# Two softmaxes without a step between maximum and exponential, and a later first product with the values

## The chip, the cores and the metric

The kernel runs on one core of one Trainium2 chip. The metric is device time in microseconds (us), from the start of one execution to its end. Three runs of the kernel before took 3143.63, 3155.43 and 3157.5 us; the median is 3155.43 us.

## The reference, cut to what matters

The model is an encoder of two layers over 1024 tokens of width 1024, all in float32. Each layer has two attention branches from one modulated input, a gated merge of them, and a channel mixer. Only the two softmaxes and their products with the values matter here.

```python
# branch A: neighbourhood attention, 8 heads of 64, window of 8 rows x 16 columns, learned bias
s = jnp.einsum('bhcd,ibhcjd->bhcij', q_r, k_nb).astype(jnp.float32) * scale      # scale = 64 ** -0.5 = 0.125
s = s + bias.transpose(0, 2, 1, 3)[None].astype(jnp.float32)
p = jax.nn.softmax(s.reshape(B, H, GRID_W, kh * kw), axis=-1)
out = jnp.einsum('bhcij,ibhcjd->bhcd', p, v_nb)

# branch B: latent attention, 8 heads, every token against all 1024 keys
q = (rmsnorm(c_q, g_q) @ w_uq).reshape(B, S, H, MLA_NOPE_DIM + MLA_ROPE_DIM)
s = (jnp.einsum('bhqd,bkhd->bhqk', qn_b, k_nope) + jnp.einsum('bhqr,bkr->bhqk', qr_b, k_r))
p = jax.nn.softmax(s.astype(jnp.float32) * scale, axis=-1)                      # scale = 96 ** -0.5
out = jnp.einsum('bhqk,bkhd->bqhd', p, v)
```

## The kernel before, in words

Each layer runs in stages: the projections; branch A with the gate products between its units; branch B; the merge; the output projection; the mixer. TensorE (PE) does all products. Most are in three parts, high and low halves of operands split by ScalarE (ACT) and VectorE (DVE) (`split`, L200; `mm3`, L204).

**Branch A** (`na_steps`, L541) has 64 units a layer, one for 128 queries of one head. `unit_a` (L595) makes 128 x 384 scores in PSUM (tile `sna`, two products, L601). One DVE operation (L605) adds the table of biases and takes the row maximum; a second, small one (L607) multiplies the maximum by -0.125; ACT takes the exponential with it as bias and leaves the row sum (L608); DVE inverts the sum (L609) and GpSimd (POOL) multiplies the tile by it (L610). `unit_b` (L613), called two units later, turns the tile in three transposes on PE (L618, `pTna`) and copies it out of PSUM, on DVE (L621) for one half of the units and on ACT (L623) for the other; there are 7 buffers for the copies. `unit_c` (L626) multiplies the values by the copies, 64 output rows for each of two heads (L632, `pona`). It is called twice after every fourth unit, so four copies feed one block of 12 products. A product of these plain float32 operands stands as two MATMUL rows in the trace: a block is 24 rows.

**Branch B** (`mla_steps`, L646) has 64 units a layer as well. `unit_a` (L790) makes 128 x 1024 scores in six products (L796, `smla`; two PSUM buffers), takes the row maximum on DVE (L798), multiplies it by minus the scale in a small DVE operation (L799), and takes the exponential on ACT with that bias and the scale (L801); then follow the inverse (L802, DVE) and the product with it (L803, POOL). `unit_b` (L806), three units later in the program, turns the tile in two times four transposes (L815, `pTm`), copied by ACT (L821) and DVE (L819) into a `PT` tile, of which there are three; two units share one. `unit_c` (L823) multiplies the values by two `PT` tiles, one for each head: 16 products (L830, `pom`), 32 MATMUL rows, for four units and so eight copies. Here too each product writes 64 rows of the output, the heads in turn.

The order of each engine's instructions is not the order of the program. A planner lays them out ahead of time by a model of durations: of the instructions whose inputs are ready in the model, it takes the one that stands first in the program. A product of a block enters PE's order when its own copy is done in that model, whether or not the other copies of the block are.

Of the kernel before, what the change touches and what calls it, by code (L numbers as in the profile page):

```python
# [13 lines left out]
ALU = mybir.AluOpType  # L14
# [23 lines left out]
def hybrid_trunk(  # L38
# [161 lines left out]
    def split(dst_hi, dst_lo, src, pin=lambda ins: ins):  # L200
        pin(A.copy(dst_hi, src))  # L201
        V.tensor_tensor(dst_lo, src, dst_hi.bitcast(F32), op=ALU.subtract)  # L202

    def mm3(ps, terms, first=True, **kw):  # L204

        n = len(terms)
        for i, (wh, wl, mh, ml) in enumerate(terms):
            T.matmul(ps, wh, mh, start=first and i == 0, stop=False, **kw)  # L208
            T.matmul(ps, wh, ml, start=False, stop=False, **kw)  # L209
            T.matmul(ps, wl, mh, start=False, stop=i == n - 1, **kw)  # L210
# [144 lines left out]
    ada_sum(acc0, first_shift[:5], 0, pin)  # L355
    turn_rows(ta, na_, 0)
    turn_rows(tb, nb_, 128)

    ada_turn(0, 1, acc1)
    last = ada_sum(acc0, first_shift[5:], 5, pin)  # L360
# [180 lines left out]
    def na_steps(l, h):  # L541

        tabs = {}
        for hd in range(2):
            for rg in range(2):
                t = pool["na"].tile([P, 12, 96], F32, name=nm(f"tab{hd}{rg}"))
                G.memset(t, NEG)
                tabs[hd, rg] = t

        def tables(pair, hd, rg):  # L550
            for r in range(8):
                row = 8 * rg + r
                st = min(max(row - 4, 0), 8)
                d0 = st - row + 7
                k0 = st - 4 * rg
                nc.sync.dma_start(tabs[hd, rg][r * 16:(r + 1) * 16, k0:k0 + 8, :], u_d[2 * pair + hd, :, d0:d0 + 8, :])

        st, vts = {}, {}

        def qk_weights(pair, n):  # L560
            st["w"] = whalves(kblock(w_in[l], (4 * n + pair) * P))

        def qk_unit(pair, n, ch):
            if ch == 0:
                st[pair, n] = [slab("st", dt=F32R) for _ in range(2)]
            ps = dense(st["w"], h[ch])
            for hd in range(2):
                dst = st[pair, n][hd][:, cs(ch)]
                if n == 0:
                    view = lambda t: t.rearrange("p (g r c) -> p r g c", g=4, c=16)  # L570
                    stacks(dst, ps[:].rearrange("p (r g c) -> p r g c", g=4, c=16), hd, view)
                else:
                    stacks(dst, ps, hd)

        def k_swap(pair):
            st[pair, 2] = [slab("st", dt=F32R) for _ in range(2)]
            for hd in range(2):
                swapped(st[pair, 2][hd], st[pair, 1][hd])

        def values(pair):  # L580
            vt = []
            for wi, w in enumerate(NA_WIN):
                if wi % 2 == 0:
                    vs = slab("vna", (P, 2, 4, P))
                for blk in range(4):
                    nc.sync.dma_start(
                        vs[:, wi % 2, blk, :],
                        v_d[:].rearrange("(b r c) d -> b r c d", r=4, c=64)[blk, :, w:w + 32, pair * P:(pair + 1) * P],
                    )
                vt.append(vs[:, wi % 2])  # L590
            vts[pair] = vt

        pts, po = {}, {}

        def unit_a(pair, rg, cg, hd):  # L595
            q1, k1, k2 = (st[pair, n][hd] for n in range(3))
            w = NA_WIN[cg]
            ps = pool["na_ps"].tile([P, 12, 32], F32, tag="S", name=nm("sna"))
            qs = q1[:, rg * CH + cg * P:rg * CH + (cg + 1) * P]
            for i, kk in enumerate((k1, k2)):  # L600
                T.matmul(ps, qs, kk[:].rearrange("p (r c) -> p r c", c=64)[:, 4 * rg:4 * rg + 12, w:w + 32],  # L601
                         start=i == 0, stop=i == 1)
            pt = pool["na"].tile([P, 12, 32], F32, tag="P", name=nm("pna"), bufs=4)
            sm = small()
            V.tensor_tensor_reduce(pt, ps, tabs[hd, rg][:, :, NA_KIND[cg] * 32:(NA_KIND[cg] + 1) * 32],  # L605
                                   op0=ALU.add, op1=ALU.max, scale=1.0, scalar=-3e38, accum_out=sm[:, 0:1])
            V.tensor_scalar(sm[:, 1:2], sm[:, 0:1], -0.125, None, op0=ALU.mult)  # L607
            A.activation(pt, pt, AF.Exp, bias=sm[:, 1:2], scale=0.125, accum_out=sm[:, 2:3])  # L608
            V.reciprocal(sm[:, 3:4], sm[:, 2:3])  # L609
            G.tensor_scalar(pt, pt, sm[:, 3:4], 1.0, op0=ALU.mult, op1=ALU.mult)  # L610
            pts[pair, rg, cg, hd] = pt

        def unit_b(pair, rg, cg, hd):  # L613
            pt = pts[pair, rg, cg, hd]
            pT = bank("pTna")
            pf = pt[:].rearrange("p a b -> p (a b)")
            for j in range(3):
                T.transpose(pT[:, j * P:(j + 1) * P], pf[:, j * P:(j + 1) * P], ident)  # L618
            t = pool["na"].tile([P, 384], F32, tag="pT", name=nm("ptna"), bufs=7)
            if (cg + hd) % 2:  # L620
                V.tensor_copy(t, pT[:, :384])  # L621
            else:
                A.copy(t, pT[:, :384])  # L623
            pts[pair, rg, cg, hd] = t

        def unit_c(pair, rg, cg):  # L626
            if cg == 0:
                po[pair, rg] = pool["na_ps"].tile([P, CH], F32, tag="po", name=nm("pona"))
            p = po[pair, rg]
            for j in range(3):  # L630
                for hd in range(2):
                    T.matmul(p[64 * hd:64 * hd + 64, cg * P:(cg + 1) * P],  # L632
                             vts[pair][cg][:, j + rg, 64 * hd:64 * hd + 64],
                             pts[pair, rg, cg, hd][:, j * P:(j + 1) * P], start=j == 0, stop=j == 2)
            if cg == 3:
                o = tmp("ona")
                V.tensor_copy(
                    o[:].rearrange("p (r g c) -> p r g c", g=4, c=16),
                    p[:].rearrange("p (g r c) -> p r g c", g=4, c=16),
                )  # L640
                nc.sync.dma_start(o_d[pair * P:(pair + 1) * P, cs(rg)], o)

        return qk_weights, qk_unit, k_swap, values, tables, unit_a, unit_b, unit_c


    def mla_steps(l):  # L646
# [138 lines left out]
                stacks(st[pair, hd][1][:, cs(ch)], ps, hd)  # L785
                swapped(st[pair, hd][2][:, cs(ch)], st[pair, hd][1][:, cs(ch)])

        pts, pTs, po = {}, {}, {}

        def unit_a(pair, q2, hd, qi):  # L790
            q1, k1, k2, qr = st[pair, hd]
            t = slice(q2 * 256 + qi * P, q2 * 256 + (qi + 1) * P)
            ps = pool["S"].tile([P, 1024], F32, tag="S", name=nm("smla"))
            for ch in range(2):
                for i, (a, b) in enumerate(((q1, k1), (q1, k2), (qr, d["Kr"]))):
                    T.matmul(ps[:, cs(ch)], a[:, t], b[:, cs(ch)], start=i == 0, stop=i == 2)  # L796
            sm = small()
            V.reduce_max(sm[:, 0:1], ps, axis=AX.X)  # L798
            V.tensor_scalar(sm[:, 1:2], sm[:, 0:1], -MLA_SCALE, None, op0=ALU.mult)  # L799
            pt = pool["mla"].tile([P, 1024], F32, tag="P", name=nm("pmla"), bufs=5)  # L800
            A.activation(pt, ps, AF.Exp, bias=sm[:, 1:2], scale=MLA_SCALE, accum_out=sm[:, 2:3])  # L801
            V.reciprocal(sm[:, 3:4], sm[:, 2:3])  # L802
            G.tensor_scalar(pt, pt, sm[:, 3:4], 1.0, op0=ALU.mult, op1=ALU.mult)  # L803
            pts[pair, q2, hd, qi] = pt

        def unit_b(pair, q2, hd, qi):  # L806
            pt = pts[pair, q2, hd, qi]
            if qi == 0:
                pTs[pair, q2, hd] = pool["mla_t"].tile([P, 8, 256], F32, tag="PT", name=nm("PT"), bufs=3)
            pT = pTs[pair, q2, hd]  # L810
            for g in range(2):
                pb = bank("pTm")
                for j in range(4):
                    kk = 4 * g + j
                    T.transpose(pb[:, j * P:(j + 1) * P], pt[:, kk * P:(kk + 1) * P], ident)  # L815
                dst = pT[:, 4 * g:4 * g + 4, qi * P:(qi + 1) * P]
                src = pb[:].rearrange("p (a b) -> p a b", b=P)
                if g:
                    V.tensor_copy(dst, src)  # L819
                else:  # L820
                    A.copy(dst, src)  # L821

        def unit_c(pair, q2, half, o):  # L823
            if half == 0:
# [2 lines left out]
            for kk in range(4 * half, 4 * half + 4):  # L827
                for hd in range(2):
                    h = 2 * pair + hd
                    T.matmul(p[64 * hd:64 * hd + 64, :256], vm[kk][:, h * 64:(h + 1) * 64], pTs[pair, q2, hd][:, kk, :],  # L830
                             start=kk == 0, stop=kk == 7)
            if half == 1:
                t = slice((q2 % 2) * 256, (q2 % 2 + 1) * 256)
                if pair == 3:
# [711 lines left out]
```

## Time and profile before

| | us |
|---|---|
| median of three runs | 3155.43 |
| profiled execution | 3154.83 |
| its span | 3153.0 |
| PE busy | 3033.6 (96%) |
| PE weight loads busy | 2456.0 (78%) |
| DVE busy | 2069.4 (66%) |
| ACT busy | 1471.2 (47%) |
| POOL busy | 373.0 (12%) |

The profiled execution is 0.6 us under the median, and 1.8 us of it lie outside the span. PE has most work in every stage. The ends of its instructions are modelled and overlap, so the distance from one start to the next tells more than a duration: a row of 0.65 us may be followed 0.57 us after its start. Rows of the view by time merge neighbours of one kind; x30 is thirty MATMUL rows in a run without another kind between them.

### The profile page before, as it was taken

The page shows a single profiled execution, that of the slowest core. Times are in us where ns is not written, and L with a number is a line of the kernel's source. Part 1 is how long each engine was busy: PE and PEld are TensorE (multiplying, and loading weights), DVE is VectorE, ACT ScalarE, POOL GpSimd, SP SyncE. Part 2 cuts the span into 40 slices and gives each one's busy share as a digit, 9 for nine tenths or more (in the row PEclk, how much of TensorE's full clock was granted, in tenths as well). Part 3 has the DMA queues.
Part 4 walks back from the last instruction along what each step waited for, and adds up shares of the span by engine and source line. Part 5 has one row for each costly group of instructions (what it writes and reads, how often), then busy time and mean ns, then how long its engine had stood idle before and what let it go on. Part 6 is the DMA issues. An engine that isn't in the chain of part 4 may idle for free. (4 is left out here: it accounts for less than half of the span.)

```text
span 3153.0 us, 43333 instructions
## 1 busy us (share of the span) xinstructions
PE 3033.6 (96%) x15104; PEld 2456.0 (78%) x15104; DVE 2069.4 (66%) x3911; ACT 1471.2 (47%) x2820; POOL 373.0 (12%) x518
## 2 busy tenths in 40 slices
PE   7999999999998999999989999999999999999998
PEld 6878886776786888888777788777777778888887
DVE  8534436767859776877774334466775697767775
ACT  6234446554127666433352444555522466663332
POOL 5111002232200000000011011123221000000000
PEclk9999999999999999999999999999999999999999
DMA  6554334214853656856334444431266255586652
GB/s 258 157 135 111 99 109 119 63 36 145 280 191 107 244 207 231 293 196 209 106 121 138 125 121 114 117 86 36 73 214 218 69 180 214 211 308 205 215 166 84
DMA packets 359540, 497.56 MB, mean 158 GB/s; under 512 B 30556, under 2 KB 238618, under 8 KB 359322
## 3 DMA queue, kind: packets, MB, share of 16 engines
q1 hardware_dynamic: 359322, 494.80, 48.9%
q8 instruction: 119, 1.95, 0.3%
q14 instruction: 99, 0.81, 0.1%
HBM read 335.41 MB, written 141.98 MB: 151 GB/s over the span
## 5 line engine op out<-in xcount | busy, mean ns | idle before, releaser
L208 PE MATMUL pd<-h,wh 128*128 128x512 f32 x768 | 307.0, 400 | 0.6 <-ACT wh L201 0.6
L210 PE MATMUL pd<-h,wh 128*128 128x512 f32 x768 | 300.7, 392 | 0.0
L209 PE MATMUL pd<-h,wh 128*128 128x512 f32 x768 | 300.1, 391 | 0.0
L208 PE MATMUL pxz<-ho,wq 128*128 128x512 f32 x672 | 259.9, 392 | 3.5 <-DVE xT L1401 3.0
L209 PE MATMUL pxz<-ho,wq 128*128 128x512 f32 x672 | 261.8, 390 | 0.5 <-DVE ho L1153 0.5
L210 PE MATMUL pxz<-ho,wq 128*128 128x512 f32 x672 | 257.0, 389 | 0.0
L201 ACT CAST wq<-s 128x512 fp32r<-128x512 f32 (+3 forms) x296 | 154.5, 541 | 125.5 <-PE pxz L210 54.2
L208 PE MATMUL px<-h,wq 128*128 128x512 f32 x512 | 202.2, 396 | 3.5 <-ACT u L1242 2.3
L1401 DVE SCALAR_TENSOR_TENSOR xT<-pxz,mod,xT 128x512 f32<-128x512 f32 x252 | 186.7, 744 | 28.4 <-PE pxz L210 28.3
L798 DVE TENSOR_REDUCE sm<-smla 128x1 f32<-128x1024 f32 x128 | 156.6, 1223 | 69.7 <-PE smla L796 63.3
L209 PE MATMUL px<-h,wq 128*128 128x512 f32 x512 | 200.2, 392 | 1.4 <-DVE h L202 1.4
L210 PE MATMUL px<-h,wq 128*128 128x512 f32 x512 | 199.6, 391 | 0.0
L801 ACT ACTIVATE pmla<-smla,sm 128x1024 f32<-128x1024 f32 x128 | 143.0, 1117 | 118.2 <-DVE sm L799 113.3
L803 POOL TENSOR_SCALAR pmla<-pmla,sm 128x1024 f32<-128x1024 f32 x128 | 144.6, 1130 | 330.4 <-DVE sm L799 153.7
L202 DVE TENSOR_TENSOR wq<-s,wq 128x512 fp32r<-128x512 f32 (+3 forms) x296 | 168.7, 582 | 6.9 <-ACT wq L201 6.9
L796 PE MATMUL smla<-st,st 128*128 128x512 f32 x512 | 170.4, 413 | 2.9 <-ACT pmla L801 2.9
L208 PEld LDWEIGHTS pd<-h,wh 128*128 128x128 f32 x768 | 144.9, 189 | 32.4 <-issue 3.4
L210 PEld LDWEIGHTS pd<-h,wh 128*128 128x128 f32 x768 | 144.6, 188 | 32.8 <-issue 1.0
L209 PEld LDWEIGHTS pd<-h,wh 128*128 128x128 f32 x768 | 145.1, 189 | 28.3
L201 ACT CAST wq<-wr 128x384 fp32r<-128x384 f32 (+3 forms) x218 | 114.7, 539 | 106.2 <-PE pxz L210 62.6
L209 PE MATMUL pyz<-h,wq 128*128 128x512 f32 x384 | 151.6, 395 | 8.0 <-DVE h L202 8.0
L208 PEld LDWEIGHTS pxz<-ho,wq 128*128 128x128 f32 x672 | 126.1, 188 | 36.3 <-issue 4.8
(281 smaller groups left out, 7344.3 us busy)
## 6 DMA issues: line engine op xcount, KB each, us to landing
hid_d<-diff SPq DMA_DIRECT2D x112, 512.0 KB
ho<-hid_d SPq DMA_DIRECT2D x112, 512.0 KB
wada<-in_w_ada_dram SPq DMA_DIRECT2D x96, 512.0 KB
wr<-in_w_ff_dram SPq DMA_DIRECT2D x64, 512.0 KB
w<-in_w_in_dram SPq DMA_DIRECT2D x56, 512.0 KB
wr<-in_w_ff_dram SPq DMA_DIRECT2D x64, 384.0 KB
ho<-hid_d SPq DMA_DIRECT2D x84, 256.0 KB
hid_d<-u SPq DMA_DIRECT2D x68, 256.0 KB
```

The costliest lines, as they stand in the source:

```text
L201: pin(A.copy(dst_hi, src))
L202: V.tensor_tensor(dst_lo, src, dst_hi.bitcast(F32), op=ALU.subtract)
L208: T.matmul(ps, wh, mh, start=first and i == 0, stop=False, **kw)
L209: T.matmul(ps, wh, ml, start=False, stop=False, **kw)
L210: T.matmul(ps, wl, mh, start=False, stop=i == n - 1, **kw)
L796: T.matmul(ps[:, cs(ch)], a[:, t], b[:, cs(ch)], start=i == 0, stop=i == 2)
L798: V.reduce_max(sm[:, 0:1], ps, axis=AX.X)
L801: A.activation(pt, ps, AF.Exp, bias=sm[:, 1:2], scale=MLA_SCALE, accum_out=sm[:, 2:3])
L803: G.tensor_scalar(pt, pt, sm[:, 3:4], 1.0, op0=ALU.mult, op1=ALU.mult)
L1401: V.scalar_tensor_tensor(x, ps, gate_m[:, nt:nt + 1], x, op0=ALU.mult, op1=ALU.add)
```

## The change

The small DVE operation goes out of both softmaxes. In branch A the fused operation writes -0.125 times the sum and takes its minimum, and the exponential runs with scale -1. In branch B the maximum is written with its sign turned, and the scale is multiplied into the four columns of gains `g_q` once, at the start. Besides, the first product of each accumulation (`j == 0`, `kk == 0`) gets an edge for the planner to every copy of its block. The edge is for the order alone (`NoSync`): it adds no wait on the chip.

```diff
+    def after_all(ins, others):
+        for o in others:
+            tc.add_manual_dep(ins.ins, o.ins.name, mybir.DependencyInfo(mybir.DependencyClass.NoSync, mybir.DependencyReason.DATA),
+                              reason="one run of the products with the values")
...
+    gq = cols[:, col0["g_q"]:col0["g_q"] + 2 * depth]
+    V.tensor_scalar(gq, gq, MLA_SCALE, None, op0=ALU.mult)
...
             V.tensor_tensor_reduce(pt, ps, tabs[hd, rg][:, :, NA_KIND[cg] * 32:(NA_KIND[cg] + 1) * 32],
-                                   op0=ALU.add, op1=ALU.max, scale=1.0, scalar=-3e38, accum_out=sm[:, 0:1])
-            V.tensor_scalar(sm[:, 1:2], sm[:, 0:1], -0.125, None, op0=ALU.mult)
-            A.activation(pt, pt, AF.Exp, bias=sm[:, 1:2], scale=0.125, accum_out=sm[:, 2:3])
+                                   op0=ALU.add, op1=ALU.min, scale=-0.125, scalar=3e38, accum_out=sm[:, 0:1])
+            A.activation(pt, pt, AF.Exp, bias=sm[:, 0:1], scale=-1.0, accum_out=sm[:, 2:3])
...
+                    if j == 0:
+                        after_all(mm, [turned[pair, rg, c, e] for c in (cg // 2 * 2, cg // 2 * 2 + 1) for e in range(2)])
...
-            V.reduce_max(sm[:, 0:1], ps, axis=AX.X)
-            V.tensor_scalar(sm[:, 1:2], sm[:, 0:1], -MLA_SCALE, None, op0=ALU.mult)
+            V.reduce_max(sm[:, 0:1], ps, axis=AX.X, negate=True)
...
-            A.activation(pt, ps, AF.Exp, bias=sm[:, 1:2], scale=MLA_SCALE, accum_out=sm[:, 2:3])
+            A.activation(pt, ps, AF.Exp, bias=sm[:, 0:1], accum_out=sm[:, 2:3])
...
+                    if kk == 0:
+                        after_all(mm, turned[pair, q2])
```

`turned` holds the copies of `unit_b`, by unit in branch A and by block in branch B.

## Rows read from the trace of the kernel before

**Rows 1.** The page, busy time and share of the span by engine.
```profile
PE 3033.6 (96%) x15104; PEld 2456.0 (78%) x15104; DVE 2069.4 (66%) x3911; ACT 1471.2 (47%) x2820; POOL 373.0 (12%) x518
```

**Rows 2.** Windows of layer 0: branch A, then branch B; window, its length, busy times.
```profile
186.70:520.40 333.70, 327.57 (x1765) 263.38 (x1763) 145.14 (x405) 161.63 (x340) 38.12 (x64) 0.98 0.45 124
520.40:764.70 244.30, 235.73 (x1485) 175.41 (x1486) 166.96 (x313) 133.12 (x234) 72.28 (x64) 1.00 0.19 54
```

**Rows 3.** Groups by line: both small operations; count, busy, mean ns.
```profile
L799 DVE TENSOR_SCALAR sm<-sm 128x1 f32<-128x1 f32 x128 | 18.5, 144 | 1.0
L607 DVE TENSOR_SCALAR sm<-sm 128x1 f32<-128x1 f32 x128 | 18.1, 148 | 0.8
```

**Rows 4.** Order of time on PE, branch B: a block in two pieces.
```profile
570.75 1.09 PE L815 MATMUL pTm<-ident,pmla 128*128 128x128 f32 x8 [0.54 <-POOL pmla L803]
571.77 0.65 PE L830 MATMUL pom<-PT,vmla 128*64 128x256 f32 x2
572.34 0.72 PE L796 MATMUL smla<-st,st 128*128 128x512 f32 x2
...
573.93 3.67 PE L830 MATMUL pom<-PT,vmla 128*64 128x256 f32 x30
577.52 0.74 PE L796 MATMUL smla<-st,st 128*128 128x512 f32 x2
```

**Rows 5.** The same view, a block in one piece.
```profile
558.55 1.03 PE L815 MATMUL pTm<-ident,pmla 128*128 128x128 f32 x8
559.52 3.67 PE L830 MATMUL pom<-PT,vmla 128*64 128x256 f32 x32
563.12 0.74 PE L796 MATMUL smla<-st,st 128*128 128x512 f32 x2
...
564.65 1.36 PE L815 MATMUL pTm<-ident,pmla 128*128 128x128 f32 x11
```

**Rows 6.** The same view, layer 1: the last block that begins with two rows.
```profile
2251.10 0.65 PE L830 MATMUL pom<-PT,vmla 128*64 128x256 f32 x2
```

**Rows 7.** Order of time on PE, branch A: a block in three pieces.
```profile
294.31 0.65 PE L632 MATMUL pona<-ptna,vna 128*64 128x128 f32 x6
294.89 0.55 PE L618 MATMUL pTna<-ident,pna 128*128 128x128 f32 x3
295.37 0.66 PE L632 MATMUL pona<-ptna,vna 128*64 128x128 f32 x8
...
298.00 0.87 PE L632 MATMUL pona<-ptna,vna 128*64 128x128 f32 x10
```

**Rows 8.** The same view, a block in one piece.
```profile
369.70 1.53 PE L632 MATMUL pona<-ptna,vna 128*64 128x128 f32 x24
```

**Rows 9.** Waits on PE: waiter, releaser, us in total, times, longest.
```profile
PE pTm L815 <- POOL pmla L803: 13.6, 29, 1.6
PE pTna L618 <- POOL pna L610: 6.9, 6, 1.7
...
PE smla L796 <- ACT pmla L801: 2.9, 2, 1.4
```

**Rows 10.** Waits on PE's weight loads, the same columns.
```profile
PEld pona L632 <- issue: 16.5, 70, 0.4
PEld pom L830 <- issue: 12.3, 46, 0.4
```

**Rows 11.** Order of time on DVE and ACT, one unit of branch B.
```profile
564.92 1.23 DVE L798 TENSOR_REDUCE sm<-smla 128x1 f32<-128x1024 f32 x1 [0.38 <-PE smla L796]
566.06 0.68 DVE L819 COPY PT<-pTm 128x512 f32<-128x512 f32 x1
...
566.65 0.14 DVE L799 TENSOR_SCALAR sm<-sm 128x1 f32<-128x1 f32 x1
...
566.89 1.12 ACT L801 ACTIVATE pmla<-smla,sm 128x1024 f32<-128x1024 f32 x1 [0.97 <-DVE sm L799]
...
569.25 0.15 DVE L802 RECIPROCAL sm<-sm 128x1 f32<-128x1 f32 x1
```

More of the change, by code (lines that the diff above doesn't have):

```diff
@@ L591, in values @@
             vts[pair] = vt
-        pts, po = {}, {}
+        pts, po, turned = {}, {}, {}
         def unit_a(pair, rg, cg, hd):
@@ L619, in unit_b @@
             t = pool["na"].tile([P, 384], F32, tag="pT", name=nm("ptna"), bufs=7)
[L620 to L623, printed above, removed]
+            copy = V.tensor_copy if (cg + hd) % 2 else A.copy
+            turned[pair, rg, cg, hd] = copy(t, pT[:, :384])
             pts[pair, rg, cg, hd] = t
@@ L631, in unit_c @@
                 for hd in range(2):
-                    T.matmul(p[64 * hd:64 * hd + 64, cg * P:(cg + 1) * P],
-                             vts[pair][cg][:, j + rg, 64 * hd:64 * hd + 64],
-                             pts[pair, rg, cg, hd][:, j * P:(j + 1) * P], start=j == 0, stop=j == 2)
+                    mm = T.matmul(p[64 * hd:64 * hd + 64, cg * P:(cg + 1) * P],
+                                  vts[pair][cg][:, j + rg, 64 * hd:64 * hd + 64],
+                                  pts[pair, rg, cg, hd][:, j * P:(j + 1) * P], start=j == 0, stop=j == 2)
+                    if j == 0:
+                        after_all(mm, [turned[pair, rg, c, e] for c in (cg // 2 * 2, cg // 2 * 2 + 1) for e in range(2)])
             if cg == 3:
@@ L786, in prep_k @@
                 swapped(st[pair, hd][2][:, cs(ch)], st[pair, hd][1][:, cs(ch)])
-        pts, pTs, po = {}, {}, {}
+        pts, pTs, po, turned = {}, {}, {}, {}
         def unit_a(pair, q2, hd, qi):
@@ L817, in unit_b @@
                 src = pb[:].rearrange("p (a b) -> p a b", b=P)
[L818 to L821, printed above, removed]
+                copy = V.tensor_copy if g else A.copy
+                turned.setdefault((pair, q2), []).append(copy(dst, src))
         def unit_c(pair, q2, half, o):
@@ L829, in unit_c @@
                     h = 2 * pair + hd
-                    T.matmul(p[64 * hd:64 * hd + 64, :256], vm[kk][:, h * 64:(h + 1) * 64], pTs[pair, q2, hd][:, kk, :],
-                             start=kk == 0, stop=kk == 7)
+                    mm = T.matmul(p[64 * hd:64 * hd + 64, :256], vm[kk][:, h * 64:(h + 1) * 64], pTs[pair, q2, hd][:, kk, :],
+                                  start=kk == 0, stop=kk == 7)
+                    if kk == 0:
+                        after_all(mm, turned[pair, q2])
             if half == 1:
```

## The prediction

> **What bounds the kernel now.** I read the page's busy times first: PE is busy 96% of the span and the next engine, DVE, 66% [rows 1]. So what counts is time on PE, and an edit on another engine counts only where PE waits for it. Then the windows of the two stages that the change touches, in layer 0: branch A lasts 333.7 us with PE idle in 6.1, branch B 244.3 us with PE idle in 8.6 [rows 2]; layer 1 repeats both within 2 us. All idle time of PE in the stages of the change is thus about 2 x 14.7 = 29 us. The third view is PE's order of time, for "busy" also holds what a change from one kind of product to another costs. The reader is to see in it the distances from start to start: the same 8 transposes, 32 value rows and 6 score products take 577.52 - 570.75 = 6.77 us where the value rows stand as 2 and 30 [rows 4], and 564.65 - 558.55 = 6.10 us where they stand as 32 [rows 5]. The fourth is the list of waits, for PE's on the softmax's chain: 13.6 us on POOL in branch B and 6.9 in branch A, both layers [rows 9].
>
> **The change part by part.** The durations come from the profiled execution, so gains and losses are summed against its 3154.83 us (span 3153.0 and 1.8 around it), 0.6 us under the median of the runs.
>
> *The small operation.* 128 of 144 ns and 128 of 148 ns leave DVE, 36.6 us of busy time [rows 3]. On DVE, at two thirds, that is worth nothing by itself. Its worth is in the chain from scores to transposes. In the unit shown the maximum ends at 564.92 + 1.23 = 566.15; the small operation stands behind a copy of 0.68 us, begins at 566.65, and ACT begins at 566.89 [rows 11]. Without it ACT can begin about 0.1 us after the maximum, so some 0.6 us earlier here, and 0.25 us where no copy stands between. ACT is busy 133 of 244 us [rows 2] and can begin earlier. What is late next is the inverse: the sum is there at about 568.1, yet L802 begins at 569.25, because the next maximum and a copy stand ahead of it on DVE [rows 11]. So a part of what the exponential wins is lost in DVE's order again. I take half of the 13.6 us in branch B, 6.8, and a third of the 6.9 in branch A, 2.3 (there the chain is shorter and gate products fill PE). The ends are nothing, if the inverse stays behind the same maximum, and all 20.5 us.
>
> *The turned maximum, the minimum, the scales.* The same instructions on the same shapes with another sign or constant. No row shows these forms, so from both sides: the 256 operations could differ by some tens of ns either way, as the two small ones differ by 4 ns [rows 3]; DVE's third of idle time hides that. I take nothing. The scaling of four columns is one operation, about 0.15 us by the small operations [rows 3], at the start, where the first modulation is made on DVE: 0.2 us lost at most.
>
> *The first products of branch B.* A block that is split as 2 and 30 costs 6.77 - 6.10 = 0.67 us more than one in one piece [rows 4, 5]. Sixteen blocks of 32 begin with a lone first product, eight in each layer at the same places; the last is at 2251.10 [rows 4, 6]. That product is of the first head, whose copies are done early, and the planner takes it while the second head's last unit is still turned. Behind all eight copies it can't, and when it is let in the other fifteen are ready too. The score products that follow it now would stand ahead: in both layers PE waited for a free buffer of theirs (ACT's exponential) only twice, 2.9 us [rows 9]. So 16 x 0.67 = 10.7 us. Six more blocks are broken farther in (22 and 10, or 26 and 6), by score products that stand earlier in the program; the edge doesn't forbid that, so I count nothing for them, and 6 x 0.67 = 4 us as the far end.
>
> *The first products of branch A.* Sixteen blocks a layer stand in 43 pieces, 27 too many, counted along the order of time (the first rows of one such block are shown [rows 7]); the list of weight loads shows the cut as well, with 70 idle moments before value rows in branch A and 46 in branch B, 0.24 and 0.27 us each, in which no semaphore was waited for ("issue") [rows 10]. The price: pieces of 6, 8 and 10 rows last 0.65 + 0.66 + 0.87 = 2.18 us, one of 24 lasts 1.53 [rows 7, 8]. Less some 0.07 that each overlaps with what follows, two more pieces cost 0.51, or 0.25 each. The three transposes ahead of a piece take 295.37 - 294.89 = 0.48 us, where eight take 0.97 [rows 5, 7], 0.12 each: 0.12 more. So 0.37 for a piece; branch B's 0.67 is the other end. With 54 pieces too many, 20 us if all go. All four first products of a block now come after all four copies, and the twelve are then ready at once; but transposes and scores of the units before them in the program may still break in once, so I let half go: 27 x 0.37 = 10.0 us, between 0 and 36.
>
> The Trainium skill says, in "TensorEngine Tiling (Array Packing)", Key Properties, that a change of the tiling mode drains TensorE; value products write 64 rows and all others 128, so each piece means two such changes. "TensorE: Matmul & The Clock Gate", Single matmul latency, puts a drain at about 175 ns; an estimate by these is 0.35 us for a piece, or 5.6 us where I have 10.7 and 9.5 where I have 10.0. The trace has 0.67 and 0.37, so the rule holds as a lower bound and the rows decide.
>
> *What the later products cost.* The edge adds no wait on the chip. Queued behind a late block are the scores and transposes that follow on PE, and the copies whose buffers it holds: 7 in branch A, three `PT` in branch B. Behind it wait DVE's and ACT's copies and, through them, PSUM. A little will be lost, above all at the end of branch A, where few gate products are left to stand in. No row shows it. I take 5 us, between nothing and 15 (half of PE's present idle time).
>
> The sum: 6.8 + 2.3 + 10.7 + 10.0 - 0.2 - 5 = 24.6 us gained. 3154.8 - 24.6 = 3130 us.
>
> **The rivals.** *A: only the sixteen go.* Branch A's blocks stay in pieces, as the planner fills in older work there at every gap, and the inverse stays behind the same maximum. Then 10.7 + some 3 - 3 = 11 us: 3144. For it: gate products, 24 rows at a time, stand in the midst of the blocks. Against: it is the early first products that open most of the pieces.
>
> *B: pieces cost nothing.* If PE's busy time were all work, at most the 29 us of idle time could go, and the edges would buy none of it; only the waits would, 9.1 - 5 = 4 us: 3151. For it: the lone product fills time in which the second head is still copied. Against: distances of 6.77 and 6.10 us for the same work, and no wait of the score products in the slow one. The skill's "Perfetto Trace Analysis", Identifying the Most-Contended Engine, says likewise that busy share of matmuls isn't the measure and that of weight loads is. Here that is 175.4 of 244.3 us, 72%, against 96% [rows 2], which speaks against B.
>
> *C: slower, late blocks hold the buffers.* A unit of branch B lasts 244.3 / 64 = 3.8 us. A block holds two of three `PT` tiles; the third lasts for two units, 7.6 us. Behind one group of scores (1.6 us) a block ends 5.2 us after the transposes and that holds. From the point where the planner lets two groups and eight transposes in ahead (5.2 + 1.6 + 1.0 = 7.8 us) the next copy waits, PSUM stays full and PE stands still, 0.2 us and the 0.97 of eight transposes that then have nothing beside them [rows 5], 1.2 us for each of 32 blocks: 38 us lost, against 24.6 gained, 3168. Against it: the planner takes what stands first in the program, and a block stands ahead of the second group.
>
> *D: more.* All pieces and all waits go, 10.7 + 4 + 20 + 20.5 - 5 = 50 us: 3105.
>
> **How the numbers follow.** The forecast, 17 to 36 us gained, has 0.50; A 0.22; B 0.13; D 0.08; C 0.07. The predicted time is the forecast's, 3130. The range takes in the forecast, all of A and half of the ground to D: 3108 to 3148; outside lie C, most of B and half of D, 0.2 together. What a measurement can tell from no change is 0.5%, 15.8 us. Faster by more: the forecast, D, and a third of A, 0.66. Within: the rest of A, B and a little of C, 0.28. Slower: 0.06.
>
> **What would show it.** Right: no block of branch B that begins with 2 rows, and 6.1 us where 6.77 stood; at most 32 pieces a layer in branch A; both small operations gone, and ACT's exponential 0.1 us behind the maximum; POOL's waits on PE under 12 us; branch B some 9 us shorter in each layer, branch A some 3 to 5. Wrong: pieces of the same number at other places (A); pieces gone and windows as long as before, the time turned into waits for copies or PSUM (B); waits of the transposes' copies on value products (C). The forecast also falls if stages after the attention, untouched by the edits, change by more than 3 us each.

## The result and the profile after

The changed kernel takes 3108.51 us (median of 5 runs, 3103.96 to 3113.54) against 3155.43: a ratio of 0.9856, interval 0.9842 to 0.9871, so 1.4% faster. The profiled execution takes 3111.81 us, its span 3110.0. That is 43.0 us less than the profiled execution before, where the prediction summed 24.6.

The windows of the four stages after, in the order branch A and B of layer 0, then of layer 1; the columns are those of [rows 2]: length, busy times (PE, its weight loads, DVE, ACT, POOL, with the number of instructions), the granted clock of TensorE as a share of 2.4 GHz, and the DMA's share and GB/s.

```profile
189.30:516.90 327.60, 320.61 (x1764) 262.96 (x1763) 137.96 (x341) 157.57 (x340) 38.93 (x64) 0.98 0.45 125
516.90:745.80 228.90, 225.13 (x1486) 175.57 (x1486) 162.04 (x249) 132.76 (x234) 72.21 (x64) 1.00 0.21 58
1713.10:2041.30 328.20, 321.08 (x1764) 263.57 (x1763) 138.11 (x341) 157.97 (x340) 38.94 (x64) 0.98 0.46 126
2041.30:2270.20 228.90, 225.15 (x1485) 175.52 (x1486) 162.04 (x249) 132.60 (x234) 72.24 (x64) 1.00 0.21 58
```

Layer 1 of the kernel before, branch A and B, for comparison:

```profile
1735.40:2067.20 331.80, 326.49 (x1763) 262.63 (x1761) 145.04 (x405) 161.56 (x340) 38.14 (x64) 0.99 0.45 125
2067.20:2311.30 244.10, 235.82 (x1485) 175.47 (x1486) 166.99 (x313) 133.00 (x234) 72.30 (x64) 1.00 0.19 54
```

The reader is to see three things. Branch B is 15.4 us shorter in layer 0 (244.30 before) and 15.2 in layer 1: 31 of the 43 us. Of the 15.4, PE's busy time gave 10.6 (235.73 to 225.13) with the same instructions, and its idle time 4.8. Branch A is 6 us shorter in layer 0 and 4 in layer 1, and PE is idle for longer there, 7.0 us where it was 6.1. The rest of the program makes up under 3 us.

The order of time on PE in branch B; the rows answer to [rows 4, 5].

```profile
577.86 1.03 PE L822 MATMUL pTm<-ident,pmla 128*128 128x128 f32 x8
578.83 3.67 PE L835 MATMUL pom<-PT,vmla 128*64 128x256 f32 x32
582.43 0.73 PE L804 MATMUL smla<-st,st 128*128 128x512 f32 x2
...
591.65 3.67 PE L835 MATMUL pom<-PT,vmla 128*64 128x256 f32 x32
```

From this block to the next, at 591.65, are 12.82 us; before, a four-unit cycle took 14.07 (571.77 to 585.84, the next block of that kind). Fourteen of sixteen blocks in a layer stand whole, where five did, and none begins with two rows. Branch A has 24 pieces in a layer instead of 43.

The waits on PE, which answer to [rows 9]:

```profile
PE sna L610 <- DVE sm L614: 6.0, 2, 3.6
...
PE pTm L822 <- POOL pmla L810: 5.2, 4, 1.5
PE pTna L626 <- POOL pna L618: 3.7, 4, 1.2
```

The wait for POOL fell from 13.6 to 5.2 us, under the 12 that the prediction named. The first row has grown: scores of branch A wait 6.0 us in both layers together for the fused operation of an earlier unit, where it was 3.6.

One unit of branch B on DVE and ACT, which answers to [rows 11]:

```profile
573.63 1.23 DVE L806 TENSOR_REDUCE sm<-smla 128x1 f32<-128x1024 f32 x1 [0.43 <-PE smla L804]
...
574.95 1.12 ACT L808 ACTIVATE pmla<-smla,sm 128x1024 f32<-128x1024 f32 x1 [0.36 <-DVE sm L809]
...
576.19 0.16 DVE L809 RECIPROCAL sm<-sm 128x1 f32<-128x1 f32 x1
576.52 1.13 POOL L810 TENSOR_SCALAR pmla<-pmla,sm 128x1024 f32<-128x1024 f32 x1 [0.29 <-DVE sm L809]
```

The maximum ends at 574.86 and the exponential begins 0.09 us later, where 0.74 us lay between. (As its releaser the row names DVE's last event, the inverse of another unit.) From the maximum's start to POOL's start are 2.89 us; in the unit of [rows 11], where POOL began at 569.56, they were 4.64. These two units differ by more than most: over all 128 units the mean fell from 4.37 to 3.54 us, 0.72 of it between maximum and exponential (0.92 to 0.20).

### The profile page after: what moved, and what is told of

It is laid out like the page before. It is cut to its first block, busy times and chain, and to the rows that moved or that the text cites. A ratio compares the mean times of both kernels' runs of the same rounds, so it can differ in the third digit from the quotient of the medians.

```text
span 3110.0 us, 43060 instructions
## 1 busy us (share of the span) xinstructions
PE 2996.7 (96%) x15104; PEld 2455.1 (79%) x15104; DVE 2050.7 (66%) x3656; ACT 1464.0 (47%) x2820; POOL 373.3 (12%) x518
## 5 line engine op out<-in xcount | busy, mean ns | idle before, releaser
L529 DVE TENSOR_SCALAR gate<-pd,cols 128x512 f32<-128x512 f32 x64 | 48.0, 751 | 166.3 <-PE pd L216 163.4
```

## The experiments

Lengths of a stage are from the profile of one execution: branch A from its first score product to branch B's first, branch B from there to its last value product. Branch B repeats within 1 us. Branch A without any edit had 333.4 and 331.9 us in the two layers of the kernel before, and 333.9, 334.1, 332.0 and 331.6 in two runs that leave it alone and have the same order on PE.

Much of that spread is TensorE's clock. A few stretches of branch A stand at a granted clock of 0.50, which is 1.2 GHz, and their number differs from run to run. The longest one of each layer in the changed kernel:

```profile
217.20:227.30 10.10, 8.52 (x38) 6.26 (x39) 5.80 (x15) 7.45 (x18) 1.76 (x3) 0.50 0.54 147
1743.00:1749.70 6.70, 6.32 (x28) 4.92 (x28) 3.02 (x7) 4.20 (x10) 1.50 (x3) 0.50 0.60 163
```

With half of the time at 1.2 GHz taken off, the six unedited stages come to 328.2 to 329.0 us. Lengths "at one clock" below are meant so. They are an estimate, which takes the engine to do half as much there. Branch B stands at 1.00 in every run but one, that with the operation twice.

**The softmaxes alone.** The change without its edges:

```diff
-                    if j == 0:
-                        after_all(mm, [turned[pair, rg, c, e] for c in (cg // 2 * 2, cg // 2 * 2 + 1) for e in range(2)])
...
-                    if kk == 0:
-                        after_all(mm, turned[pair, q2])
```

> Both softmaxes as in the change, no edge on any value product. Theory 1, the steps of the prediction: the edges join the blocks of value products, and the shorter softmax takes only some waits off PE (9.1 us); then branch B lasts about 240 us in each layer (244 before, 229 after), branch A about 332, and the whole 3146. Theory 2: the shorter softmax joins branch B's blocks by itself, because the planner, with the small operation gone from its model, finds the next scores ready ahead of the block; the edges do nothing there. Its order on PE has 36 pieces of value products in branch B, as the change has (54 before), and 76 in branch A (86 before, 48 after). Then branch B lasts 229 us in each layer as after, branch A loses 10 pieces of 0.37 us, and the whole is about 3155 - 31 - 4 - 2 = 3118.

Measured: 3116.69 us, ratio 0.987 (0.9847 to 0.9893). Branch A and B of layer 0, then branch A of layer 1:

```profile
189.10:520.20 331.10, 325.80 (x1763) 263.93 (x1761) 138.75 (x341) 158.79 (x340) 37.68 (x64) 0.99 0.45 123
520.20:749.10 228.90, 225.11 (x1485) 175.60 (x1486) 162.06 (x249) 132.72 (x234) 72.21 (x64) 1.00 0.21 59
1720.50:2048.20 327.70, 323.20 (x1763) 262.09 (x1761) 138.58 (x341) 158.77 (x340) 37.67 (x64) 1.00 0.45 125
```

Branch B has the length after, 228.9 us, to the tenth, with no edge in the kernel. Theory 1 falls.

**The edges alone.** The edges of the change on the kernel before, both softmaxes as they were.

> The edges on the first products in both branches, both softmaxes as before. Theory 1: sixteen lone products go in branch B, 10.7 us, and half of the pieces in branch A, 10.0 us: 3134, branch B about 239 us in each layer. Theory 2: the planner's order of branch B keeps all 54 pieces, since its lone products stood behind all copies already and were cut off by scores that stand earlier in the program; branch B stays at 244 us, branch A goes from 86 pieces to 48, 38 x 0.37 = 14 us at most, in the profile about the 10 us that the change shows there: 3141 to 3145.

Measured: 3140.86 us, ratio 0.9951 (0.9935 to 0.9967). Branch B:

```profile
512.70:756.90 244.20, 235.83 (x1488) 175.62 (x1486) 166.60 (x313) 132.99 (x234) 72.25 (x64) 1.00 0.19 54
```

and a block in it, on three engines in the order of time:

```profile
563.39 0.59 ACT L826 COPY PT<-pTm 128x512 f32<-128x512 f32 x1 [0.69 <-PE pTm L822]
...
563.72 0.65 PE L835 MATMUL pom<-PT,vmla 128*64 128x256 f32 x2
563.83 0.69 DVE L826 COPY PT<-pTm 128x512 f32<-128x512 f32 x1
...
565.88 3.67 PE L835 MATMUL pom<-PT,vmla 128*64 128x256 f32 x30
```

The lone product stands where it stood, cut off from its block by scores, and on the chip it starts 0.11 us before the last copy of its block does: the edge neither moved it in PE's order nor made it wait. Branch A went to 330.8 us in both layers, 4 us together for 38 pieces fewer. But 27.3 us of it stand at 1.2 GHz, where it was 17.1 in the kernel before; at one clock the two stages are 8.9 us shorter, near the 10 that were expected. The median is 15.7 us under that of the runs of before beside it (3156.56). Some of the rest lies in stretches that the edges don't touch: before branch A this profile has 182.0 us, those of the eight other changed kernels 188.7 to 189.3 and the kernel before 186.9, with the same order on PE. Of these 4.9 us, 3.4 are the clock by the same estimate (6.8 us at 1.2 GHz against 13.7). At one clock about 5 us of the profiled execution, outside both branches, stay unexplained.

**Blocks whole, the small operation kept.** The kernel before, with one edge in branch B, to the scores of the unit emitted last:

```diff
-                    T.matmul(ps[:, cs(ch)], a[:, t], b[:, cs(ch)], start=i == 0, stop=i == 2)
+                    scored["b"] = T.matmul(ps[:, cs(ch)], a[:, t], b[:, cs(ch)], start=i == 0, stop=i == 2)
...
+                    if kk == 0:
+                        after_all(mm, [scored["b"]])
```

> The kernel before with one edge more: the first value product of a block of branch B stands behind the scores of the unit emitted last. Small operation, durations and branch A as before; the 54 pieces of branch B become 32. If a cut costs PE 0.67 us whatever else happens (the price in the prediction), 22 cuts go and 14.7 us with them: 3140, branch B about 237 us in each layer. If the lone products only filled time in which PE would have waited for the softmax, branch B stays within 2 us of 244 and PE's waits for POOL grow from 13.6 us to over 25: 3155. In between, what is missing of the 15.4 us that the change gains in each layer's branch B is the share of the shorter chain.

Measured: 3134.65 us, ratio 0.9932 (0.9915 to 0.995). Branch B in both layers:

```profile
522.70:757.80 235.10, 227.45 (x1486) 173.22 (x1486) 165.88 (x313) 133.19 (x234) 72.27 (x64) 1.00 0.19 56
...
2061.60:2296.20 234.60, 227.42 (x1487) 173.43 (x1486) 165.98 (x313) 133.13 (x234) 72.31 (x64) 1.00 0.20 56
```

9.2 and 9.5 us went for 11 cuts in each layer, 0.85 us a cut, and 8.3 of the 9.2 out of busy time. The scores stand in about as many groups as before (129, and 127 before, in both layers together). So cuts cost PE time that the profile counts as busy, with the softmax as it was; rival B falls.

**A version with all blocks whole.** The change with more edges:

```diff
-                        after_all(mm, [turned[pair, rg, c, e] for c in (cg // 2 * 2, cg // 2 * 2 + 1) for e in range(2)])
+                        after_all(mm, [turned[pair, rg, c, e] for c in (cg // 2 * 2, cg // 2 * 2 + 1) for e in range(2)] + [scored["a"], scored["t"]])
...
-                        after_all(mm, turned[pair, q2])
+                        after_all(mm, turned[pair, q2] + [scored["b"]])
```

`scored` holds the last score product of either branch and the last transpose of branch A.

> The change with more edges: in branch B the first products also stand behind the scores emitted last, in branch A also behind the scores and transposes emitted last. 32 pieces in branch B instead of 36, 38 in branch A instead of 48. By the prices of the prediction 4 x 0.67 + 10 x 0.37 = 6.4 us faster than the change: 3102 where the change has 3108.5. If late blocks hold buffers (rival C), branch A grows longer than the 328 us after and the whole is 3109 or more.

Measured: 3100.33 us, ratio 0.9822 (0.9807 to 0.9837), an interval wholly below that of the change: it beats both kernels. Layer 0:

```profile
188.80:514.10 325.30, 317.76 (x1763) 262.17 (x1762) 137.76 (x341) 157.66 (x340) 39.24 (x64) 0.99 0.46 126
514.10:739.30 225.20, 223.35 (x1487) 175.30 (x1486) 161.19 (x249) 132.68 (x234) 72.28 (x64) 1.00 0.21 59
```

With 32 whole blocks in both, branch B has 225.2 us here and 234.9 with the small operation: 9.7 us a layer go with the operation, beside the 9.3 of the cuts. Of the 9.9 in layer 0, 5.8 are idle time of PE (7.65 to 1.85) and 4.1 busy time with the same instructions (227.45 to 223.35). Branch A did not grow, so rival C does not show.

**The small operation beside the chain.** The softmaxes alone, with the operation still issued but read by nobody:

```diff
             V.reduce_max(sm[:, 0:1], ps, axis=AX.X, negate=True)
+            ghost = V.tensor_scalar(sm[:, 1:2], sm[:, 0:1], -MLA_SCALE, None, op0=ALU.mult)
...
-            A.activation(pt, ps, AF.Exp, bias=sm[:, 0:1], accum_out=sm[:, 2:3])
+            after_all(A.activation(pt, ps, AF.Exp, bias=sm[:, 0:1], accum_out=sm[:, 2:3]), [ghost])
```

and the same in branch A.

> As the run with both softmaxes alone (3116.7 us), but the small DVE operation is still issued in each unit of both branches, into a column that nobody reads; the exponential takes the value of the fused or turned maximum and doesn't wait for it. DVE has its 36.6 us of work back, the chain from scores to transposes stays short, and the planner's blocks are the same (36 pieces in branch B, 76 in branch A). If the chain was what counted: branch B 229 us in each layer, 3117 for the whole. If DVE's load counted: branch B goes back towards 244, in proportion 3135 to 3150.

Measured: 3117.36 us, ratio 0.9881 (0.9866 to 0.9895); branch B 229.5 and 229.8 us. Layer 0, and one unit with the operation beside the chain:

```profile
519.50:749.00 229.50, 225.58 (x1485) 175.58 (x1486) 166.43 (x313) 132.84 (x234) 72.21 (x64) 1.00 0.20 57
```

```profile
563.99 1.23 DVE L805 TENSOR_REDUCE sm<-smla 128x1 f32<-128x1024 f32 x1 [0.54 <-PE smla L803]
...
565.25 0.15 DVE L806 TENSOR_SCALAR sm<-sm 128x1 f32<-128x1 f32 x1
565.31 1.12 ACT L808 ACTIVATE pmla<-smla,sm 128x1024 f32<-128x1024 f32 x1 [0.37 <-DVE sm L805]
```

The exponential begins 0.09 us after the maximum ends, while the small operation still runs. As work on DVE the operation is worth 0.6 to 0.9 us a layer; what counts is its place between maximum and exponential, in the planner's model and on the chip.

**The operation twice.** Blocks whole with the small operation kept, and a second one behind it:

```diff
-            V.tensor_scalar(sm[:, 1:2], sm[:, 0:1], -MLA_SCALE, None, op0=ALU.mult)
+            V.tensor_scalar(sm[:, 2:3], sm[:, 0:1], -1.0, None, op0=ALU.mult)
+            V.tensor_scalar(sm[:, 1:2], sm[:, 2:3], MLA_SCALE, None, op0=ALU.mult)
```

> As the run in which branch B's blocks are whole with the small operation kept (3134.7 us, branch B 234.9 us in each layer), but with two small operations one after the other between maximum and exponential in branch B. Still 32 whole blocks. With none of them, the run with whole blocks had 225.2 us. If PE waits at the transposes for the length of this chain, the second operation costs about what the first did, 9.7 us a layer: branch B 244 us, 3154 for the whole. If the first one only tipped the planner's order over, the second costs under 3 us a layer: 3135 to 3140.

Measured: 3160.61 us, ratio 1.0019 (1.001 to 1.0029). Branch B in both layers, then the longest wait on PE:

```profile
520.70:764.20 243.50, 229.54 (x1487) 174.41 (x1486) 173.82 (x377) 133.70 (x234) 72.30 (x64) 0.99 0.19 54
...
2068.80:2319.10 250.30, 233.86 (x1487) 177.50 (x1486) 172.49 (x377) 133.80 (x234) 72.16 (x64) 0.97 0.18 52
```

```profile
PE smla L803 <- ACT pmla L809: 17.5, 9, 3.2
```

The second operation costs 8.4 and 15.7 us, the first 9.7. The wait has moved on, from the transposes to the scores, which wait for the exponential to free one of their two buffers: 17.5 us, where 4.9 stood with one operation. One layer loses 7 us more than the other, and 4.3 of these stand as busy time with the same instructions (229.54 and 233.86). That goes with the clock. Layer 1 has 13.7 us at 1.2 GHz, in three stretches, each of which begins within 1 us of the end of such a wait of about 3 us; layer 0 has one of 3.4 us. Two pairs of score products, the second behind a wait and at the lower clock:

```profile
2257.40 0.71 PE L803 MATMUL smla<-st,st 128*128 128x512 f32 x2
...
2263.93 1.22 PE L803 MATMUL smla<-st,st 128*128 128x512 f32 x2 [3.15 <-ACT pmla L809]
```

```profile
2263.20:2269.90 6.70, 5.97 (x16) 4.70 (x17) 2.12 (x6) 1.77 (x4) 2.22 (x2) 0.50 0.24 73
```

At one clock the second operation costs 6.7 and 9.0 us. Why layer 1 has more of these waits, 11.1 us against 6.5, is open; the planner's orders of the two layers differ in places.

**Blocks cut in two.** The change with the second half of each block called one unit later:

```diff
-                for half in range(2):
-                    mla["c"](pair, q2, half, o)
+                mla["c"](pair, q2, 0, o)
+            if j >= 4 and j % 4 == 1:
+                pair, q2, _, _ = order[j - 2]
+                mla["c"](pair, q2, 1, o)
```

> The change with the second half of each block in branch B called one unit later in the program, so that scores and transposes get in between: 76 pieces of value products there instead of 36, everything else as in the change (3108.5 us, branch B 229 us in each layer). If a cut costs PE what the whole blocks won (18.6 us for 22 cuts, 0.85 us each, or 0.67 by the rows of before), 40 cuts cost 27 to 34 us: branch B 242 to 246 us, 3135 to 3142. If whole blocks won because the scores came earlier and not because of the cut, branch B stays within 4 us of 229: 3108 to 3116.

Measured: 3128.09 us, ratio 0.9913 (0.9898 to 0.9928).

```profile
517.50:755.70 238.20, 236.76 (x1487) 176.08 (x1486) 159.89 (x249) 131.33 (x234) 72.39 (x64) 1.00 0.20 55
```

The change had 228.90 us here, 225.13 of them busy. Branch B is 9.3 us longer in each layer for 20 cuts, and PE is idle for less, 1.4 us against 3.8: all of it is busy time. A cut costs 0.46 us here, less than expected. The scores stand in 106 groups instead of 126 in both layers together, so some changes between scores and transposes went as those to value rows came.

**No edges in branch A.** The version with all blocks whole, without `after_all` in branch A.

> The fastest kernel so far (3100.3 us) without the edges in branch A: 76 pieces there instead of 38, branch B's 32 whole blocks kept (225 us in each layer). By the price of the prediction, 0.37 us a piece, branch A gets 14 us longer in both layers together and the whole is 3114. By what the first runs show (28 pieces fewer, some 3 us), 0.1 us a piece, 4 us: 3104.

Measured: 3106.4 us, ratio 0.9849 (0.9834 to 0.9864). Branch A in the kernels of this case, layer 0 and layer 1, in us:

| kernel | pieces | length | of it at 1.2 GHz | at one clock |
|---|---|---|---|---|
| before | 86 | 333.4, 331.9 | 10.2, 6.8 | 328.3, 328.5 |
| edges alone | 48 | 330.8, 330.8 | 13.7, 13.7 | 324.0, 323.9 |
| softmaxes alone | 76 | 331.1, 327.7 | 6.8, 0 | 327.7, 327.7 |
| no edges in A | 76 | 331.2, 327.7 | 6.8, 0 | 327.8, 327.7 |
| the change | 48 | 327.6, 328.1 | 10.2, 10.2 | 322.4, 323.0 |
| blocks of B cut in two | 48 | 328.6, 323.5 | 10.2, 3.4 | 323.4, 321.8 |
| all blocks whole | 38 | 325.3, 322.1 | 6.8, 0 | 321.8, 322.1 |

The two layers of the run with all blocks whole and of this one had the same time at 1.2 GHz, so they can be compared as they stand: 38 pieces are worth 11.5 us, 0.30 each, between both expectations.

The edges of the change seem to be worth less: 331.1 and 327.7 against 327.6 and 328.2 us, 3.0 us for 28 pieces. Two things take from them. PE's idle time goes from 5.3 and 4.5 us to 7.0 and 7.1, 4.3 more. And 20.5 us stand at 1.2 GHz where it was 6.8, by the estimate another 6.8 us. At one clock the edges are worth 10.0 us, 0.36 a piece. The time at 1.2 GHz isn't fixed by the order: the run with blocks of branch B cut in two has branch A in the same order on PE as the change, instruction for instruction, and layer 1 is 4.6 us shorter there. The whole runs put the edges at 4 to 8 us (ratios 0.987 and 0.9856, medians 3116.69 and 3108.51).

In the change the two long stretches at 1.2 GHz, from 217.2 and 1742.9 us, begin in or just behind the wait that had grown, that of branch A's scores for the fused operation:

```profile
218.47 1.01 PE L610 MATMUL sna<-st,st 128*128 128x384 f32 x2 [3.61 <-DVE sm L614]
...
1741.01 0.63 PE L610 MATMUL sna<-st,st 128*128 128x384 f32 x2 [2.35 <-DVE sm L614]
```

## Why the prediction was right, and where it was not

*The sign, the range and the bound.* What counts is PE's time in the two branches, and cuts hide in its busy time: shown. The median lies 0.5 us within the low end, and that is luck: 24.6 us were summed and 43.0 measured in the profile, and the two terms of branch B miss in opposite directions, by 10.5 and 23.7 us.

*The first products of branch B: 10.7 us predicted, 0.2 measured.* This step failed. "Behind all eight copies it can't" take the lone product ahead, the prediction said. With the edges alone all sixteen lone products stayed. I had read the cause of the cut from the wrong side: the product stood behind its block's copies already, and what cut it off was the next scores, which come earlier in the program and became ready just after it. An edge to those scores makes all blocks whole with the softmax as it was. In the changed kernel the sixteen did go, as forecast, but by the shorter softmax; that this sign came out right is luck too.

*The small operation: 6.8 us predicted in branch B, 30.5 measured.* This is the mis-sized term. I priced it by the waits on PE alone, half of 13.6 us [rows 9]. The runs show two effects. With the operation gone the planner joins nine of eleven cut blocks a layer by itself; at the 0.85 us of a cut that is about 7.7 of the 15.3 us. The remainder goes with the operation's place in the chain, worth 9.7 us a layer when all blocks are whole. The wait list had held only a part of that: PE's idle time at transposes. The prediction also feared that DVE's order would take a part back at the inverse; over all 128 units the time from the exponential's end to POOL's start fell too, from 1.11 to 1.00 us. How much of the 9.7 the chip's shorter chain gives and how much the planner's new order (scores of just two units in a row in 14 places of both layers, where there was none) is not settled: no run had the one without the other. That 4.1 of the 9.9 in layer 0 are busy time points to the order for a part. The operation twice shows only that length goes on costing.

*Branch A: 10.0 for the edges and 2.3 for the softmax, less 5 of new waits, 7.3 in all; 9.5 measured.* The sum is near. As the lengths stand, the terms are not: the softmax alone gives 6.5, the edges 3.0 net. At one clock, by the estimate, the softmax gives 1.4 and the edges 10.0, with the idle time that they brought already taken off; so the softmax was near, the edges were priced too low, and most of the 6.5 was the clock. Pieces are worth 0.23 (edges alone) to 0.36 us net of new waits, near the 0.37 of [rows 7, 8]; the new wait, bounded between nothing and 15, is 4.3 us of idle time, at the scores. That the clock fell at such a wait the prediction did not have.

*The drain.* By "TensorEngine Tiling (Array Packing)", Key Properties, in the Trainium skill, a change of the tiling mode drains TensorE. The runs agree in that a cut of branch B, with two such changes, costs busy time: 0.85 us saved, 0.46 us when it takes the place of another switch. What each change of kind costs alone, and whether the drain is the cause, no run here shows. In branch A a piece can be worth less, net of waits, than the 0.35 us that the prediction took for a lower bound.

*The rivals.* A (only the sixteen go) falls by branch A, where 24 pieces stand instead of 43, and by the softmaxes alone; B (cuts are free) falls by whole blocks with the chain kept. C, late blocks that hold the buffers, did not come: in both branches blocks still later were faster still. The gain, 43 us in the profile, lies between the forecast's 17 to 36 and D's 50, and D, with 0.08 of the chances, was the nearer on the blocks that are broken farther in: one of the three in a layer went, which I had counted at nothing. The stretch between the attentions of both layers, several stages long, changed by 3.3 us (970.6 to 967.3), as it does between kernels that leave it alone (964.4 to 973.0; at one clock 955.9 to 959.4).

## What to carry to other kernels

Where a planner sets the order ahead of time, an edit changes two things, the chain on the chip and the order on every engine: compare both orders, edit by edit, before pricing anything, as an edge can do nothing and an arithmetic detail can join blocks. A small operation between two engines is priced by the chain it lengthens, and a list of waits on the bound engine is no upper end for that price, since lost time also stands as cuts within "busy". To test such an edit, put the operation beside the chain, and put it in twice. Before a difference of a few us in one stage is given to an edit, compare the granted clock of the two stages.

## What the runs showed of the hardware that was not expected

256 operations of 0.146 us left DVE, 37 us by their durations [rows 3], but its busy time fell by 18.7 us only (2069.4 to 2050.7) and by 24 in the four windows: their records overlap with their neighbours', as the copy at 566.06 and the small operation at 566.65 do [rows 11]. Without the records of these two lines the trace of the kernel before has 18.3 us less of busy time on DVE, about the 18.7 that went. The duration of such an operation is no measure of what the engine gets back here.

A wait on PE can cost twice. In or just behind waits of 2.4 to 3.6 us the granted clock fell from 1.00 to 0.50 in the rows shown, and two score products took 1.22 us where 0.71 stood 6.5 us earlier. That second part stands as busy time of PE and in no list of waits.
